# Batched fp32 matmul: groups of two matrices under automatic scheduling, against groups of four in hand-written engine programs with hardware loops

## The chip, the cores and the metric

One core of a Trainium2 chip. The metric is the device time of one execution in microseconds (us), as a median over runs. Ratios are the mean time of one kernel's fast runs over that of the other's in the same rounds, so they are not quite the ratio of the medians quoted beside them. "Span" is the time from the first to the last instruction in the profiled execution; the measured time is about 2 us longer.

## The reference

```python
b1, b2, m, k, n = 8, 16, 256, 512, 384
x:      (8, 16, 256, 512) float32
weight: (8, 16, 512, 384) float32
out = np.matmul(x, weight)          # 128 independent products, float32
```

168 MB are read and 50 MB written. The kernels cast to bf16 on the chip.

## The kernel before

It takes two matrices at a time (G = 2). A partition holds R = 4 consecutive rows of x of the pair, an 8 KB run. VectorE casts x to bf16, TensorE transposes it (two bf16 as one 4-byte word), VectorE copies the transposed x out of PSUM. Because each partition holds several rows, a product comes out with the matrices interleaved over partition blocks, and ScalarE needs G copies per matrix to put it in the order of the output.

```python
G = 2
C = P // G;  R = G * M // P;  J = R // G
LAG = 4                                   # stores kept back, in groups
...
def load_x(b):
    x_sb = x_pool.tile([P, R, K], fp32, name="x_sb")
    nc.sync.dma_start(x_sb[:], x_rows[b*M:(b+G)*M].rearrange("(p r) k -> p r k", r=R))
...
for b in range(0, B, G):
    last = b == B - G
    x_sb = load_x(b);  w_sb = [load_w(b + i) for i in range(G)]
    if last:
        while waiting: store()            # the kept stores go out behind the last loads
    x_t = transpose_x(x_sb)
    for i in range(G):
        ... cast of w, 8 matmuls into po ...
        mine = slice(i * C, (i + 1) * C)
        for g in range(G):
            nc.scalar.copy(out=out_sb[mine, g::G, :], in_=po[g*C:(g+1)*C, :, :N])
        if last: ... one store per matrix ...
    if not last: ... append; if len(waiting) > LAG: store() ...
```

## Time and profile before

| | before |
|---|---|
| time, median of 4 runs | 526.38 us (526.18 to 526.95) |
| span of the profiled run | 524.2 us |
| DMA share and rate, 20 to 500 us | 1.01, 423 GB/s |
| busiest compute engine | TensorE, 62% |
| data packets and semaphore packets | 36,880 |

How to read it: a share of 1.01 of 16 DMA engines means that by the records every engine has a packet under way all the time. The kernel is as fast as its DMA, plus a head in which nothing has arrived and a tail in which the last results are made and stored. The page lines for this are in the prediction below. One pair of views is shown here, because the prediction took a number from the first that the second contradicts. The first is the chain of waits at the end (start, length, what), the second VectorE's timeline in the same microseconds (start, length, what, and in brackets the idle time before and what ended it).

```profile
495.89 14.54 DMA w_sb<-in_weight_dram
510.44 0.01 issue
510.45 0.80 ACT out_sb L126
511.25 3.98 issue
```

```profile
510.21 1.23 DVE L76 CAST x_bf<-x_sb 128x2048 bf16<-128x2048 f32 x1 [3.17 <-DMA x_sb<-in_x_dram]
512.06 0.96 DVE L113 CAST w_bf<-w_sb 128x1536 bf16<-128x1536 f32 x1 [0.62 <-DMA w_sb<-in_weight_dram]
512.93 1.28 DVE L85 COPY x_t<-pt 128x1024 bf16<-128x1024 bf16 x2
514.13 0.95 DVE L113 CAST w_bf<-w_sb 128x1536 bf16<-128x1536 f32 x1
```

The chain's last DMA piece ends at 510.43. But the second view has VectorE waiting for the last **x** until 510.21, and for a weight until 512.06, with one more weight cast after that. Both weights of a group are queued behind its x, so what landed near 510 was the last x (at 510.11 us by the records of DMA completions), not the last weight.

### The profile page before, as it was taken

The page shows a single profiled execution, that of the slowest core. Times are in us where ns is not written, and L with a number is a line of the kernel's source. Part 1 is how long each engine was busy: PE and PEld are TensorE (multiplying, and loading weights), DVE is VectorE, ACT ScalarE, POOL GpSimd, SP SyncE. Part 2 cuts the span into 40 slices and gives each one's busy share as a digit, 9 for nine tenths or more (in the row PEclk, how much of TensorE's full clock was granted, in tenths as well). Part 3 has the DMA queues.
Part 4 walks back from the last instruction along what each step waited for, and adds up shares of the span by engine and source line. Part 5 has one row for each costly group of instructions (what it writes and reads, how often), then busy time and mean ns, then how long its engine had stood idle before and what let it go on. Part 6 is the DMA issues. An engine that isn't in the chain of part 4 may idle for free.

```text
span 524.2 us, 4635 instructions
## 1 busy us (share of the span) xinstructions
PE 324.2 (62%) x1536; PEld 187.1 (36%) x1536; DVE 272.8 (52%) x320; ACT 204.4 (39%) x257; POOL 0.7 (0%) x6
## 2 busy tenths in 40 slices
PE   4665665666655666657666565576646756757653
PEld 2443343333333433334333333343333433423331
DVE  4656455464554544645546456454464554645542
ACT  1462434434334343343343443424334334243342
POOL 0000000000000000000000000000000000000000
PEclk9898788887888878888788888877898888788788
DMA  8999999999999999999999999999999999999997
GB/s 342 421 414 418 421 424 422 424 422 422 425 423 421 422 422 423 423 423 422 424 422 424 421 424 424 420 425 424 424 426 424 420 425 424 425 422 425 424 423 258
DMA packets 36903, 218.40 MB, mean 417 GB/s; under 512 B 4113, under 2 KB 4113, under 8 KB 28689
## 3 DMA queue, kind: packets, MB, share of 16 engines
q1 hardware_dynamic: 36880, 218.12, 100.2%
q8 instruction: 12, 0.20, 0.1%
q14 instruction: 11, 0.08, 0.0%
HBM read 167.77 MB, written 50.33 MB: 416 GB/s over the span
## 4 chain that ended last, share of the span: by engine, by line
DMA 97%; issue 1%; ACT 1%; SPq 0%; ACTq 0%
DMA w_sb<-in_weight_dram 94%; DMA x_sb<-in_x_dram 3%; ACT out_sb L126 1%; ACTq L162 0%; SPq L66 0%; SPq L59 0%
## 5 line engine op out<-in xcount | busy, mean ns | idle before, releaser
L126 ACT COPY out_sb<-po 64x768 f32<-64x768 f32 x256 | 203.2, 794 | 313.3 <-issue 274.1
L117 PE MATMUL po<-w_bf,x_t 128*128 128x384 bf16 x1024 | 232.5, 390 | 48.1 <-DVE x_t L85 38.1
L76 DVE CAST x_bf<-x_sb 128x2048 bf16<-128x2048 f32 x64 | 78.5, 1227 | 199.0 <-DMA x_sb<-in_x_dram 199.0
L81 PE MATMUL pt<-identity,x_bf 128*128 128x128 f32 x512 | 92.2, 335 | 144.3 <-DVE x_bf L76 144.3
L117 PEld LDWEIGHTS <-x_t 128*128 128x128 bf16 x1024 | 109.7, 114 | 163.2 <-DVE x_t L85 60.1
L113 DVE CAST w_bf<-w_sb 128x1536 bf16<-128x1536 f32 x128 | 121.9, 955 | 38.6 <-DMA w_sb<-in_weight_dram 38.6
L81 PEld LDWEIGHTS pt<-identity,x_bf 128*128 128x128 f32 x512 | 77.4, 213 | 166.0 <-issue 164.9
L85 DVE COPY x_t<-pt 128x1024 bf16<-128x1024 bf16 x128 | 82.7, 684 | 4.8 <-PE pt L81 4.8
L126 ACT ACT_TABLE_LOAD x1 | 1.3, 1283 | 0.7 <-PEq L151 0.7
masks.py:199 POOL TENSOR_SCALAR_AFFINE_SELECT identity<-identity 128x128 f32<-128x128 f32 x1 | 0.3, 293 | 0.1
masks.py:197 POOL MEMSET identity<- 128x128 f32 x1 | 0.2, 204 | 0.3 <-POOLq L151 0.3
L151 POOL MEMSET const-bfloat16-1.0<- 128x1 bf16 x1 | 0.1, 102 | 0.0
L151 POOL MEMSET const-uint8-127<- 128x1 uint8 x1 | 0.1, 102 | 0.0
L151 POOL MEMSET const-float32-0.0<- 128x1 f32 x1 | 0.1, 99 | 0.2 <-issue 0.2
L151 POOL MEMSET const-float32-1.0<- 128x1 f32 x1 | 0.1, 99 | 0.0
## 6 DMA issues: line engine op xcount, KB each, us to landing
w_sb<-in_weight_dram SPq DMA_DIRECT2D x128, 768.0 KB, 16.1
x_sb<-in_x_dram SPq DMA_DIRECT2D x64, 1024.0 KB, 16.1
out_dram<-out_sb SPq DMA_DIRECT2D x63, 768.0 KB, 16.1
out_dram<-out_sb SPq DMA_DIRECT2D x2, 384.0 KB, 5.1
```

What stands on the lines that cost most here:

```text
L76: nc.vector.tensor_copy(out=x_bf[:, r0 : r0 + 4], in_=x_sb[:, r0 : r0 + 4])
L81: nc.tensor.transpose(pt[:, rr, h, :], words[:, r + rr, h :: KO // 2], identity)
L85: nc.vector.tensor_copy(out=x_t[:, j, :, :, g : g + 2].rearrange("k h i g c e -> k g (h i) (c e)"), in_=pt[:].bitcast(bf16).rearrange("k g ...
L113: nc.vector.tensor_copy(out=w_bf[:], in_=w_sb[i][:])
L117: nc.tensor.matmul(po[:, j, :N], x_t[:, j, ko // 2, i, :, :, ko % 2].rearrange("k g c -> k (g c)"), w_bf[:, ko, :], start=(ko == 0), stop= ...
L126: nc.scalar.copy(out=out_sb[mine, g::G, :], in_=po[g * C : (g + 1) * C, :, :N])
L151: nc = _bacc.Bacc("TRN2", target_bir_lowering=False, num_devices=1)
```

## The change

The intent: fewer and longer DMA packets (16 KB rows of x, 12 KB rows of out), a short program in hardware loops, and one engine, ScalarE, for all copies of results out of PSUM. The price that was known beforehand: four copies per matrix instead of two. The diff, cut to its core (each engine gets its own program, ordered by semaphores that count):

```diff
-    G = 2
+    G = 4                       # R = 8 rows per partition: 16 KB of x, 12 KB of out
     C = P // G
     R = G * M // P
-    LAG = 4
+    AHEAD = 2                   # groups of loads ahead
+    XS, WS, OS = AHEAD, AHEAD * G, 4
+    PT, PO = 4, 2               # PSUM: transposes, products (before 2 and 3)
...
+    def load(e, n, n0):
+        wait(e, x_cast, n - XS + 1)
+        e.dma_start(x_sb[n0 % XS][:], ...).then_inc(x_in[n0 % XS], 16)
+        for i in range(G):
+            wait(e, w_cast, n * G + (i + 1 - WS))
+            e.dma_start(w_sb[(n0 * G + i) % WS][:], ...).then_inc(...)
+    def store(e, n, n0):
+        e.wait_ge(o_copied, n * G + G)
+        e.dma_start(out=..., in_=out_sb[n0 % OS][:]).then_inc(o_out[n0 % OS], 16)
...
+    def copy_out(e, n, n0, t):                       # ScalarE
+        wait(e, o_out[n0 % OS], t * 16)
+        for i in range(G):
+            e.wait_ge(p_made, n * G + (i + 1))
+            for g in range(G):
+                ins = e.copy(out=out_sb[n0 % OS][i*C:(i+1)*C, g::G, :],
+                             in_=po[(n0*G + i) % PO][g*C:(g+1)*C, :, :N])
+            ins.then_inc(o_copied, 1)
...
+    @block.sync
+    def _(e):
+        for n in range(AHEAD): load(e, n, n)
+        with e.Fori(0, rounds) as t:
+            for s in range(U):
+                load(e, t * U + (AHEAD + s), AHEAD + s)
+                store(e, t * U + s, s)
+        for n in range(rounds * U, NG):
+            if n + AHEAD < NG: load(e, n + AHEAD, n + AHEAD)
+            store(e, n, n)
```

VectorE's program for a group is: cast x (one instruction), cast the first weight, four copies of transposed x, cast the other three weights. TensorE's is: 16 transposes, then four products. The special treatment of the last group (kept stores, one store per matrix) is gone.

More of the change, by code (lines that the diff above doesn't have):

```diff
@@ L27 @@
     x_rows = x.rearrange("b1 b2 m k -> (b1 b2 m) k")
+    w_rows = weight.rearrange("b1 b2 k n -> (b1 b2 k) n")
     o_rows = out.rearrange("b1 b2 m n -> (b1 b2 m) n")
-    w_flat = weight.rearrange("b1 b2 k n -> (b1 b2) k n")
     fp32 = mybir.dt.float32
     bf16 = mybir.dt.bfloat16
-    G = 2
+    G = 4
     C = P // G
@@ L39 @@
     J = R // G
-    LAG = 4
-    const = ctx.enter_context(tc.tile_pool(name="const", bufs=1))
-    x_pool = ctx.enter_context(tc.tile_pool(name="x_pool", bufs=3))
-    xb_pool = ctx.enter_context(tc.tile_pool(name="xb_pool", bufs=2))
-    xt_pool = ctx.enter_context(tc.tile_pool(name="xt_pool", bufs=2))
-    w_pool = ctx.enter_context(tc.tile_pool(name="w_pool", bufs=6))
-    wb_pool = ctx.enter_context(tc.tile_pool(name="wb_pool", bufs=4))
-    out_pool = ctx.enter_context(tc.tile_pool(name="out_pool", bufs=7))
@@ L50 @@
-    psum_t = ctx.enter_context(tc.tile_pool(name="psum_t", bufs=2, space=bass.MemoryType.PSUM))
-    psum_o = ctx.enter_context(tc.tile_pool(name="psum_o", bufs=3, space=bass.MemoryType.PSUM))
-    identity = const.tile([P, P], fp32)
-    make_identity(nc, identity)
-    def load_x(b):
-        x_sb = x_pool.tile([P, R, K], fp32, name="x_sb")
-        nc.sync.dma_start(
-            x_sb[:], x_rows[b * M : (b + G) * M].rearrange("(p r) k -> p r k", r=R)
-        )
-        return x_sb
-    def load_w(b):
-        w_sb = w_pool.tile([P, KO, N], fp32, name="w_sb")
-        nc.sync.dma_start(w_sb[:], w_flat[b].rearrange("(kp ko) n -> kp ko n", ko=KO))
-        return w_sb
@@ L69, in transpose_x @@
-    def transpose_x(x_sb):
-        x_bf = xb_pool.tile([P, R, K], bf16, name="x_bf")
-        x_t = xt_pool.tile([P, J, KO // 2, G, G, C, 2], bf16, name="x_t")
-        words = x_bf[:].bitcast(fp32)
-        for r0 in range(0, R, 4):
-            nc.vector.tensor_copy(out=x_bf[:, r0 : r0 + 4], in_=x_sb[:, r0 : r0 + 4])
-            for r in range(r0, r0 + 4, 2):
-                pt = psum_t.tile([P, 2, KO // 2, P], fp32, name="pt")
-                for rr in range(2):
-                    for h in range(KO // 2):
-                        nc.tensor.transpose(
-                            pt[:, rr, h, :], words[:, r + rr, h :: KO // 2], identity
-                        )
-                j, g = divmod(r, G)
-                nc.vector.tensor_copy(
-                    out=x_t[:, j, :, :, g : g + 2].rearrange(
-                        "k h i g c e -> k g (h i) (c e)"
-                    ),
-                    in_=pt[:].bitcast(bf16).rearrange(
-                        "k g h (i ce) -> k g (h i) ce", i=G
-                    ),
-                )
-        return x_t
@@ L95 @@
-    waiting = []
-    def store():
-        dram, out_sb = waiting.pop(0)
-        nc.sync.dma_start(out=dram, in_=out_sb)
-    for b in range(0, B, G):
-        last = b == B - G
-        x_sb = load_x(b)
-        w_sb = [load_w(b + i) for i in range(G)]
-        if last:
-            while waiting:
-                store()
-        x_t = transpose_x(x_sb)
-        out_sb = out_pool.tile([P, R, N], fp32, name="out_sb")
-        for i in range(G):
-            w_bf = wb_pool.tile([P, KO, N], bf16, name="w_bf")
-            nc.vector.tensor_copy(out=w_bf[:], in_=w_sb[i][:])
-            po = psum_o.tile([P, J, 512], fp32, name="po")
+    NG = B // G
@@ new lines, with sbuf, psum, sems @@
+    AHEAD = 2
+    XS, WS, OS = AHEAD, AHEAD * G, 4
+    BS, TS, WBS = 2, 2, 4
+    PT, PO = 4, 2
+    ctx.enter_context(tc.tile_critical())
+    def sbuf(name, shape, dtype, n):
+        return [
+            ctx.enter_context(nc.sbuf_tensor(f"{name}{s}", shape, dtype)) for s in range(n)
+        ]
+    def psum(name, shape, dtype, n):
+        return [
+            ctx.enter_context(nc.psum_tensor(f"{name}{s}", shape, dtype)) for s in range(n)
+        ]
+    def sems(name, n):
+        return [tc.alloc_semaphore(f"{name}{s}") for s in range(n)]
@@ new lines @@
+    identity = sbuf("identity", [P, P], fp32, 1)[0]
+    x_sb = sbuf("x_sb", [P, R, K], fp32, XS)
+    x_bf = sbuf("x_bf", [P, R, K], bf16, BS)
+    x_t = sbuf("x_t", [P, J, KO // 2, G, G, C, 2], bf16, TS)
+    w_sb = sbuf("w_sb", [P, KO, N], fp32, WS)
+    w_bf = sbuf("w_bf", [P, KO, N], bf16, WBS)
+    out_sb = sbuf("out_sb", [P, R, N], fp32, OS)
+    pt = psum("pt", [P, 2, KO // 2, P], fp32, PT)
+    po = psum("po", [P, J, 512], fp32, PO)
+    x_in, w_in, o_out = sems("x_in", XS), sems("w_in", WS), sems("o_out", OS)
@@ new lines, with wait @@
+    id_done, x_cast, w_cast, t_copied, t_made, p_made, o_copied = (
+        sems(name, 1)[0]
+        for name in (
+            "id_done", "x_cast", "w_cast", "t_copied", "t_made", "p_made", "o_copied"
+        )
+    )
+    T = R // 2
+    def wait(e, sem, value):
+        if not isinstance(value, int) or value > 0:
+            e.wait_ge(sem, value)
+    def load(e, n, n0):
+        wait(e, x_cast, n - XS + 1)
+        e.dma_start(
+            x_sb[n0 % XS][:],
+            x_rows[bass.ds(n * (G * M), G * M)].rearrange("(p r) k -> p r k", r=R),
+        ).then_inc(x_in[n0 % XS], 16)
+        for i in range(G):
+            wait(e, w_cast, n * G + (i + 1 - WS))
+            e.dma_start(
+                w_sb[(n0 * G + i) % WS][:],
+                w_rows[bass.ds(n * (G * K) + i * K, K)].rearrange(
+                    "(p ko) n -> p ko n", ko=KO
+                ),
+            ).then_inc(w_in[(n0 * G + i) % WS], 16)
@@ new lines, in store, with cast, cast_w @@
+    def store(e, n, n0):
+        e.wait_ge(o_copied, n * G + G)
+        e.dma_start(
+            out=o_rows[bass.ds(n * (G * M), G * M)].rearrange("(p r) n -> p r n", r=R),
+            in_=out_sb[n0 % OS][:],
+        ).then_inc(o_out[n0 % OS], 16)
+    def cast(e, n, n0, t):
+        e.wait_ge(x_in[n0 % XS], t * 16)
+        wait(e, t_made, n * T + (1 - BS) * T)
+        e.tensor_copy(out=x_bf[n0 % BS][:], in_=x_sb[n0 % XS][:]).then_inc(x_cast, 1)
+        def cast_w(i):
+            e.wait_ge(w_in[(n0 * G + i) % WS], t * 16)
+            wait(e, p_made, n * G + (i + 1 - WBS))
+            e.tensor_copy(
+                out=w_bf[(n0 * G + i) % WBS][:], in_=w_sb[(n0 * G + i) % WS][:]
+            ).then_inc(w_cast, 1)
+        cast_w(0)
+        wait(e, p_made, n * G + (1 - TS) * G)
+        for q in range(T):
+            e.wait_ge(t_made, n * T + (q + 1))
+            j, g = divmod(2 * q, G)
+            e.tensor_copy(
+                out=x_t[n0 % TS][:, j, :, :, g : g + 2].rearrange(
+                    "k h i g c e -> k g (h i) (c e)"
+                ),
+                in_=pt[(n0 * T + q) % PT][:].bitcast(bf16).rearrange(
+                    "k g h (i ce) -> k g (h i) ce", i=G
+                ),
+            ).then_inc(t_copied, 1)
+        for i in range(1, G):
+            cast_w(i)
@@ new lines, in multiply @@
+    def multiply(e, n, n0):
+        words = x_bf[n0 % BS][:].bitcast(fp32)
+        e.wait_ge(x_cast, n + 1)
+        for q in range(T):
+            wait(e, t_copied, n * T + (q + 1 - PT))
+            for rr in range(2):
+                for h in range(KO // 2):
+                    ins = e.transpose(
+                        pt[(n0 * T + q) % PT][:, rr, h, :],
+                        words[:, 2 * q + rr, h :: KO // 2],
+                        identity[:],
+                    )
+            ins.then_inc(t_made, 1)
+        e.wait_ge(t_copied, n * T + T)
+        for i in range(G):
+            e.wait_ge(w_cast, n * G + (i + 1))
+            wait(e, o_copied, n * G + (i + 1 - PO))
@@ L115 @@
             for j in range(J):
                 for ko in range(KO):
-                    nc.tensor.matmul(
-                        po[:, j, :N],
-                        x_t[:, j, ko // 2, i, :, :, ko % 2].rearrange("k g c -> k (g c)"),
-                        w_bf[:, ko, :],
+                    ins = e.matmul(
+                        po[(n0 * G + i) % PO][:, j, :N],
+                        x_t[n0 % TS][:, j, ko // 2, i, :, :, ko % 2].rearrange(
+                            "k g c -> k (g c)"
+                        ),
+                        w_bf[(n0 * G + i) % WBS][:, ko, :],
@@ L123 @@
                     )
-            mine = slice(i * C, (i + 1) * C)
-            for g in range(G):
-                nc.scalar.copy(out=out_sb[mine, g::G, :], in_=po[g * C : (g + 1) * C, :, :N])
-            if last:
-                waiting.append((o_rows[(b + i) * M : (b + i + 1) * M].rearrange(
-                    "(p r) n -> p r n", r=R), out_sb[mine]))
-                store()
-        if not last:
-            waiting.append(
-                (o_rows[b * M : (b + G) * M].rearrange("(p r) n -> p r n", r=R), out_sb[:])
-            )
-            if len(waiting) > LAG:
-                store()
+            ins.then_inc(p_made, 1)
@@ new lines, in copy_out @@
+    def copy_out(e, n, n0, t):
+        wait(e, o_out[n0 % OS], t * 16)
+        for i in range(G):
+            e.wait_ge(p_made, n * G + (i + 1))
+            for g in range(G):
+                ins = e.copy(
+                    out=out_sb[n0 % OS][i * C : (i + 1) * C, g::G, :],
+                    in_=po[(n0 * G + i) % PO][g * C : (g + 1) * C, :, :N],
+                )
+            ins.then_inc(o_copied, 1)
+    block = ctx.enter_context(nc.Block())
+    @block.gpsimd
+    def _(e):
+        e.memset(identity[:], 0.0).then_inc(id_done, 1)
+        e.wait_ge(id_done, 1)
+        make_identity(nc, identity[:], nomemset=True)
+        e.drain().then_inc(id_done, 1)
@@ new lines, in _ @@
+    @block.sync
+    def _(e):
+        U = OS
+        for n in range(AHEAD):
+            load(e, n, n)
+        rounds = (NG - AHEAD) // U
+        with e.Fori(0, rounds) as t:
[3 more added lines that the diff above has]
+        for n in range(rounds * U, NG):
+            if n + AHEAD < NG:
+                load(e, n + AHEAD, n + AHEAD)
+            store(e, n, n)
+        for s in range(OS):
+            e.wait_ge(o_out[s], 16 * (NG // OS))
@@ new lines, in _ @@
+    @block.vector
+    def _(e):
+        U = XS
+        for n in range(U):
+            cast(e, n, n, 1)
+        with e.Fori(1, NG // U) as t:
+            for s in range(U):
+                cast(e, t * U + s, s, t + 1)
+    @block.tensor
+    def _(e):
+        U = 4
+        e.wait_ge(id_done, 2)
+        for n in range(U):
+            multiply(e, n, n)
+        with e.Fori(1, NG // U) as t:
+            for s in range(U):
+                multiply(e, t * U + s, s)
+    @block.scalar
+    def _(e):
+        U = OS
+        for n in range(U):
+            copy_out(e, n, n, 0)
+        with e.Fori(1, NG // U) as t:
+            for s in range(U):
+                copy_out(e, t * U + s, s, t)
```

## The prediction

> **What bounds the kernel now.** I read the page first: the busy line, the slices, the DMA queues, the chain that ended last.
>
> ```profile
> PE 324.2 (62%) x1536; PEld 187.1 (36%) x1536; DVE 272.8 (52%) x320; ACT 204.4 (39%) x257; POOL 0.7 (0%) x6
> ...
> DMA  8999999999999999999999999999999999999997
> ...
> DMA packets 36903, 218.40 MB, mean 417 GB/s; under 512 B 4113, under 2 KB 4113, under 8 KB 28689
> ...
> q1 hardware_dynamic: 36880, 218.12, 100.2%
> ...
> DMA w_sb<-in_weight_dram 94%; DMA x_sb<-in_x_dram 3%; ACT out_sb L126 1%; ACTq L162 0%; SPq L66 0%; SPq L59 0%
> ```
>
> No compute engine is busy for more than 62% of the span, the 16 DMA engines are full in all slices but the first and the last, and 97% of the chain is loads. So the bound is the time of the DMA engines. The view by stage says how much is not steady state; its columns are length, busy time of PE, PEld, DVE, ACT, POOL, then granted clock, DMA share, GB/s.
>
> ```profile
> 0.00:2.00 2.00, 0.00 (x0) 0.00 (x0) 0.00 (x0) 1.27 (x1) 0.70 (x6) 1.00 0.21 25
> 2.00:510.50 508.50, 320.10 (x1512) 184.71 (x1512) 268.81 (x316) 199.26 (x253) 0.00 (x0) 0.85 1.01 422
> 510.50:517.00 6.50, 4.13 (x24) 2.42 (x24) 3.96 (x5) 2.48 (x4) 0.00 (x0) 1.00 0.94 390
> 517.00:524.20 7.20, 0.00 (x0) 0.00 (x0) 0.00 (x0) 1.44 (x2) 0.00 (x0) 0.78 0.53 150
> ```
>
> 508.5 of 524.2 us run at 422 GB/s. The head costs 2 us. The last weight lands at 510.45 us (chain in order of time), so the tail is 13.75 us; DMA is near full until 517, because four groups of stores were kept back for it, and half idle after.
>
> **What the Trainium skill says.** "HBM Reference", section Access: one core streaming alone measures about 425 GB/s, bounded by its 16 DMA engines. The trace agrees: 422. So only cheaper packets could speed the steady part up. "DMA: Bandwidth & Descriptors", section Why small descriptors are slow, gives each packet a fixed overhead of about 3 cycles. The trace shows such a term but larger: in its packet records the median of the 6144 B packets is 234 ns, of the 8192 B packets 309 ns, of the 4 B semaphore packets 9 ns. That is 75 ns per 2 KB and 9 ns fixed, whatever the size. "ScalarE: Activation LUTs", section What ACT_TABLE_LOAD costs, times an instruction as 186 ns + 0.833 ns per element of the free size, with no term for partitions; 768 elements would be 826 ns, less some 93 ns of overlap. The trace has 794 ns for 64x768. "Runtime: NRT & Kernel Launch", section Instruction fetch mechanics: instructions come in 16 KB blocks by DMA, and a taken branch to a block outside the window waits for a fetch. The trace has 12 instruction packets of 16 KB, of about 1.04 us each, and no loop.
>
> **The change, part by part.**
>
> Packets. Per four matrices and DMA engine, before: 16 x packets of 8 KB, 32 w of 6 KB, 16 out of 6 KB, 8 semaphore packets, 72 in all. After: 8 of 16 KB, 32 of 6 KB, 8 of 12 KB, 6 semaphores, 54. The bytes are the same. What is a fixed packet cost in throughput? Casts of x start 8.06 us apart (median of the trace), so 16.12 us per four matrices; the bytes alone are 2 x 104 units of 2 KB x 75 ns = 15.60 us; the rest, 0.52 us over 72 packets, is 7.2 ns. Eighteen fewer packets save 0.13 us, giving 15.99 us. Times 32: **-4.2 us**, 0.8%. If a 16 KB row were split into 8 KB packets, only 10 of the 18 would go and the saving would be 2.3 us; 16 KB instruction packets in this trace speak against a split.
>
> ScalarE.
>
> ```profile
> L126 ACT COPY out_sb<-po 64x768 f32<-64x768 f32 x256 | 203.2, 794 | 313.3 <-issue 274.1
> L117 PE MATMUL po<-w_bf,x_t 128*128 128x384 bf16 x1024 | 232.5, 390 | 48.1 <-DVE x_t L85 38.1
> L113 DVE CAST w_bf<-w_sb 128x1536 bf16<-128x1536 f32 x128 | 121.9, 955 | 38.6 <-DMA w_sb<-in_weight_dram 38.6
> ```
>
> With four matrices interleaved, a result leaves PSUM in four copies of 32x768, not two of 64x768. The free size is unchanged, so I take 794 ns each (0.805 apart, from 3.22 us for four in the timeline): 512 copies, 407 us, 12.9 us of each 16 us. ScalarE doubles to 77% busy and still fits. VectorE work is the same but with one cast per eight rows: from 955 ns at 1536 and 1227 ns at 2048 elements, 0.53 ns per element plus 139, so 2.31 us for 4096.
>
> Does the DMA stay fed? Times from the landing of a group's x: cast to 2.4; first weight cast to 3.4; four transposed copies at 684 ns to 6.1; first product at about 7.9; ScalarE's 16 copies to **20.8**. SyncE issues the store then, and the next group's loads behind it. In the queue at that moment lie the rest of the next group's weights, one store and a whole group of loads: the second next group ends landing at 2 x 16 + 7.4 = 39.5, so about **18 us of work are queued**. At the start, with three groups of loads and no stores, the margin is about 11 us. The wait for the store in front of the loads is therefore hidden. The loops' register work and branches lie on engines with idle time: hidden too, except in head and tail.
>
> Tail. The last weight lands at T. Before T go all loads and 29 of 32 stores (45.6 MB) against 59 of 64 (46.4 MB) now: -1.9 us. T = 510.45 - 1.9 - 4.0 = 504.6; I add 0.5 us for the entry into the blocks: 505. The last x landed 7.5 us before T, so by the same steps ScalarE ends at T + 13.3: 12.9 us of copies start just after T, because x_t was ready then. Two held stores fill the DMA to about T + 7.4, then it idles. The final 1.57 MB goes out in one piece. Now:
>
> ```profile
> 515.23 3.22 ACT L126 COPY out_sb<-po 64x768 f32<-64x768 f32 x4 [3.98 <-issue]
> ...
> 516.86 2.09 SPq L99 DMA_DIRECT2D out_dram<-out_sb  x2
> ```
>
> The last store of 0.39 MB was issued at 518.48 and the program ended 5.7 us later; its data took some 2 us. The new one needs 3.7 us of data (8 packets x 459 ns): about 7.7 us. Tail: 13.3 + 7.7 = **21 us** against 13.75, so **+7.3**.
>
> Sum: -4.2 +0.2 (part of the saving falls after T) -1.9 +7.3 +0.5 head +1 for leaving the block and for semaphore and register instructions in the last group = +2.9. Span 527; the measured time is 2.3 us above the span, so about 529 us.
>
> **The rivals.** (1) ScalarE becomes the bound. For it: 77% by my sum, only two PSUM buffers, so TensorE waits for it. Against: 12.9 of 16 us even when nothing overlaps within a group. It takes 25% more per copy to bind; then 32 x 16.1 and more, 535 to 550. (2) SyncE's wait for the store starves the loads. For it: one in-order queue. Against: the 18 us of margin; it needs a group's latency to double. Would be 540 or more. (3) The loops' branches refetch instructions by DMA. TensorE's loop is some 500 instructions, two or three blocks, seven times round: 14 to 21 blocks for the 12 of now. That adds little (0.6 us of one DMA engine each), but if all engines refetched and the fetches fell on one DMA engine, 5 to 15 us: up to 540. (4) The packet saving is larger or the DMA is fed more evenly, since the eight outstanding transfers of now (issue to landing 16.1 us for every kind, two groups) no longer limit it: at most about 5 us more, 522 to 525. DMA is already over 100% busy, so little is to be had. (5) The tail is shorter because ScalarE starts earlier than T; one or two us.
>
> **Range and chances.** Gain and loss are both below 1.5% and nearly cancel. The bytes at a pure 75 ns per 2 KB take 499 us, and head and new tail add some 20, so faster by 2% (under 516) is close to impossible. Slower by 2% (over 537) needs rival 1, 2 or 3. I put the time at 529.0 us, eight in ten between 522 and 537, 0.02 faster, 0.87 same, 0.11 slower.
>
> **What would show it.** Right: about 27,650 data and semaphore packets; 16 KB packets of about 609 and 12 KB ones of about 459 ns; x casts 15.9 to 16.1 us apart; DMA digits 9 but at the ends; 512 copies of about 794 ns; a last weight landing near 505 and a tail of about 21 us with DMA idle in its middle. Wrong: copies shorter or longer than 794 ns; DMA digits below 9 in mid-run; SyncE waiting on ScalarE with an empty queue; many more instruction packets; x casts at 16.1 or above in spite of fewer packets (then the packet cost overlaps and the saving is nil, 533).

## The result, and the profile after

532.06 us (median of 4; 531.13 to 532.20) against 526.38: ratio 1.0102, 95% interval 1.0085 to 1.0120. The time lies inside the range, but the loss is 5.7 us where +2.6 had been said (529.0 less 526.38).

The page of the changed kernel: engines, slices, packets, queue, ScalarE's copies.

```profile
PE 322.8 (61%) x1536; PEld 192.4 (36%) x1536; DVE 269.2 (51%) x288; ACT 405.5 (76%) x513; POOL 0.7 (0%) x6
...
DMA  8999999999999999999999999999999999999972
...
DMA packets 27655, 218.19 MB, mean 411 GB/s; under 512 B 3073, under 2 KB 3073, under 8 KB 19457
...
q1 hardware_dynamic: 27648, 218.12, 98.2%
...
L180 ACT COPY out_sb<-po 32x768 f32<-32x768 f32 x512 | 404.2, 789 | 117.1 <-PE po L163 110.1
```

What to see: ScalarE's work doubled as worked out (512 copies of 789 ns) and it still waits 110 us for TensorE; the DMA engines are full until the last two slices. Those two are at 7 and 2 tenths; before it was one slice at 7. So ScalarE did not become the bound of the steady part. SyncE waits long for ScalarE, but the DMA queue never runs dry in mid-run:

```profile
SPq L110 <- ACT out_sb L180: 226.2, 32, 16.6
```

That is 226 us of waiting in an in-order queue that costs nothing until the end; the backlog covers it, as the issue-to-landing time of 26 to 27 us per load (16.1 before) also says.

Now the end. By the trace's records of DMA completions, the last weight landed at **513.83 us** before and at **509.32 us** after. With the stages cut there (length, busy PE, PEld, DVE, ACT, POOL, clock, DMA share, GB/s), first before:

```profile
2.00:513.80 511.80, 321.42 (x1521) 185.86 (x1522) 271.48 (x319) 200.00 (x253) 0.00 (x0) 0.85 1.01 422
513.80:524.20 10.40, 2.81 (x16) 1.27 (x14) 1.28 (x2) 3.17 (x4) 0.00 (x0) 0.85 0.63 215
```

and after:

```profile
2.00:509.30 507.30, 315.97 (x1506) 189.31 (x1507) 266.97 (x286) 391.78 (x497) 0.00 (x0) 0.80 1.01 424
509.30:513.00 3.70, 2.59 (x16) 1.36 (x14) 2.20 (x3) 2.35 (x3) 0.00 (x0) 1.00 0.91 389
513.00:523.50 10.50, 4.25 (x16) 1.76 (x16) 0.00 (x0) 10.28 (x14) 0.00 (x0) 0.61 0.04 18
523.50:530.20 6.70, 0.00 (x0) 0.00 (x0) 0.00 (x0) 0.00 (x0) 0.00 (x0) 0.50 0.56 235
```

Before, the last weight is followed by 10.4 us. After, by 20.9 us: 3.7 in which the queue drains, **10.5 in which the DMA engines stand idle** (share 0.04) while ScalarE is busy for 10.28 of 10.50 us, and 6.7 for the last store. The gain up to the last weight is 4.5 us, the loss behind it 10.6; the span grows by 6.1 us. The packet records say what the 4.5 us are. Up to the last weight, 48.1 MB of stores had gone out before the change and 47.05 MB after it (bytes moved by then, less the loads), which at 422 GB/s are 2.4 us that were only moved behind the last weight. From the first packet on, bytes moved at 421.6 GB/s before and 423.5 after, which over 214.8 MB is a true gain of 2.3 us. The first packet came 0.2 us later. ScalarE's part of the tail is one line of its timeline, and the store that waits for it is the second of the two issues merged in SyncE's line:

```profile
510.63 12.84 ACT L180 COPY out_sb<-po 32x768 f32<-32x768 f32 x16 [3.52 <-PE po L163]
...
507.14 16.69 SPq L110 DMA_DIRECT2D out_dram<-out_sb  x2
```

The other half of the change can be read from the packet records: medians of 611 ns for 16 KB and 460 ns for 12 KB packets (609 and 459 had been worked out), and 3 instruction packets of 16 KB in place of 12.

### The profile page after: what moved, and what is told of

Same layout as the page of the kernel before. It is cut to its first block, busy times and chain, and to the rows that moved or that the text cites. A ratio compares the mean times of both kernels' runs of the same rounds, so it can differ in the third digit from the quotient of the medians.

```text
span 530.3 us, 5467 instructions
## 1 busy us (share of the span) xinstructions
PE 322.8 (61%) x1536; PEld 192.4 (36%) x1536; DVE 269.2 (51%) x288; ACT 405.5 (76%) x513; POOL 0.7 (0%) x6
## 4 chain that ended last, share of the span: by engine, by line
DMA 50%; ACT 23%; PE 9%; issue 8%; DVE 7%; SPq 1%; ACTq 0%; DVEq 0%
DMA x_sb<-in_x_dram 50%; ACT out_sb L180 23%; PE pt L151 5%; DVE x_bf L119 5%; PE po L163 4%; DVE x_t L133 2%; SPq L110 1%; ACTq _compat.py:109 0%; DVE w_bf L124 0%; SPq L95 0%; DVEq L90 0%; SPq L201 0%; DVEq L131 0%; ACTq L236 0%; ACTq L178 0%
## 5 line engine op out<-in xcount | busy, mean ns | idle before, releaser
L180 ACT COPY out_sb<-po 32x768 f32<-32x768 f32 x512 | 404.2, 789 | 117.1 <-PE po L163 110.1
L163 PE MATMUL po<-w_bf,x_t 128*128 128x384 bf16 x1024 | 226.9, 379 | 142.1 <-ACT out_sb L180 108.8
L163 PEld LDWEIGHTS po<-w_bf,x_t 128*128 128x128 bf16 x1024 | 104.8, 109 | 255.7 <-issue 204.2
L119 DVE CAST x_bf<-x_sb 128x4096 bf16<-128x4096 f32 x32 | 73.4, 2294 | 220.8 <-DMA x_sb<-in_x_dram 220.8
L151 PE MATMUL pt<-identity,x_bf 128*128 128x128 f32 x512 | 96.2, 364 | 55.0 <-DVE x_bf L119 55.0
L124 DVE CAST w_bf<-w_sb 128x1536 bf16<-128x1536 f32 x128 | 116.7, 953 | 0.0
L151 PEld LDWEIGHTS pt<-identity,x_bf 128*128 128x128 f32 x512 | 87.6, 218 | 71.1 <-issue 69.6
L133 DVE COPY x_t<-pt 128x1024 bf16<-128x1024 bf16 x128 | 84.5, 688 | 21.5 <-PE pt L151 20.9
```

What stands on the lines that cost most here:

```text
L119: e.tensor_copy(out=x_bf[n0 % BS][:], in_=x_sb[n0 % XS][:]).then_inc(x_cast, 1)
L124: e.tensor_copy(out=w_bf[(n0 * G + i) % WBS][:], in_=w_sb[(n0 * G + i) % WS][:]).then_inc(w_cast, 1)
L133: e.tensor_copy(out=x_t[n0 % TS][:, j, :, :, g : g + 2].rearrange("k h i g c e -> k g (h i) (c e)"), in_=pt[(n0 * T + q) % PT][:].bitcast( ...
L151: ins = e.transpose(pt[(n0 * T + q) % PT][:, rr, h, :], words[:, 2 * q + rr, h :: KO // 2], identity[:],)
L163: ins = e.matmul(po[(n0 * G + i) % PO][:, j, :N], x_t[n0 % TS][:, j, ko // 2, i, :, :, ko % 2].rearrange("k g c -> k (g c)"), w_bf[(n0 * G ...
L180: ins = e.copy(out=out_sb[n0 % OS][i * C : (i + 1) * C, g::G, :], in_=po[(n0 * G + i) % PO][g * C : (g + 1) * C, :, :N],)
```

## The experiments

The theories. **P**: a packet costs some 7 ns of DMA throughput, so fewer packets explain the gain up to the last weight. Its rivals: **N**, the fixed part of a packet is hidden, since the median cadence of x casts (the time from the start of one to the start of the next) barely fell (2 x 8.06 = 16.12 to 16.11 us per four matrices); and **F**, the gain comes from the loops, as instruction packets disappear. **T**: the loss is the new tail, ScalarE's copies and then the undivided store. Its rival **D**: the drain of the queue or the chain from the last x sets the end anyway.

| run | time, us | ratio to before | last weight landed | last copy ended | span |
|---|---|---|---|---|---|
| r_after | 531.14 | 1.0091 | 508.91 | 522.77 | 529.57 |
| e_unrolled | 531.65 | 1.0106 | 508.80 | 522.32 | 529.57 |
| e_pk72 | 536.07 | 1.0181 | 512.39 | 527.77 | 534.66 |
| e_pk144 | 550.04 | 1.0452 | 527.43 | 540.22 | 547.26 |
| t_split | 529.87 | 1.0062 | 509.21 | 523.16 | 528.12 |
| t_share | 528.09 | 1.0033 | 509.21 | 519.03 | 525.87 |
| t_xearly | 533.13 | 1.0130 | 509.16 | 524.65 | 531.46 |
| t_share_x | 529.00 | 1.0054 | 509.07 | 520.15 | 526.99 |
| b_order | 527.37 | 1.0016 | 509.45 | 519.03 | 525.87 |
| b_share_split | 525.74 | 0.9993 | 509.04 | 518.75 | 523.75 |
| b_share_split_2 | 525.43 | 0.9983 | 509.17 | 517.99 | 523.00 |
| b_final | 526.38 | 0.9988 | 509.39 | 519.46 | 524.47 |

The columns of landings and copies are from each run's profile. Half-widths of the ratios' 95% intervals are 0.0013 to 0.0019. All results were correct.

### The changed kernel again, and its loops unrolled

> The changed kernel again, as the base for the runs beside it: 531 to 532.2 us, cadence of the x casts 16.11 us, last weights landing near 509.3 us.

> The changed kernel with its loops unrolled, nothing else. Theory F (the hardware loops give the steady part its gain, because the instruction packets of 16 KB stop: 12 before, 3 after): 12 or more such packets come back and with them single steps of the x casts 0.4 to 0.8 us longer than the median of 16.11; the time grows by 2 to 3 us to about 534.5. Rival (the fewer data packets give the gain, the loops give nothing): time within 0.7 us of the changed kernel, 532.

```diff
-        with e.Fori(1, NG // U) as t:
+        for t in range(1, NG // U):        # likewise in all four programs
```

r_after came out at the low end of what was expected: 531.14 us, cadence 16.08 us, last weight at 508.91 us. Unrolled, the instruction packets came back. These are both pages' lines for queue q8, whose 16 KB packets are taken here for TensorE's by their number (an inference), first with loops (r_after), then unrolled:

```profile
q8 instruction: 3, 0.05, 0.0%
```

```profile
q8 instruction: 12, 0.20, 0.1%
```

The time moved by 0.5 us (by the ratios, 1.0106 against 1.0091, by 0.8 us, with intervals that overlap). **F falls at the size it claimed**, 2 to 3 us; an effect under 1 us is possible and not shown. The last weight landed at 508.80 us against 508.91, but with 0.45 MB fewer stores gone out before it: the rate up to there is 422.8 GB/s unrolled against 423.6, which is about 0.9 us, in one profile each. Two single steps of the x casts are 0.3 to 0.4 us above 16.11 in the unrolled run; the profiled run of the changed kernel, with loops, has one such step too (16.53 us), so they are no proof of a cost of fetches.

### The old packet sizes in the new kernel, and half of them

> The changed kernel with each x load in two transfers of 8 KB runs and each store in two of 6 KB runs: 72 packets per four matrices and engine as before the change, not 54. Theory P of the prediction (a packet costs 7.2 ns of throughput): 18 x 7.2 ns x 32 = +4.2 us, about 536. Rival N (the fixed part of a packet overlaps its neighbour, since the cadence fell only from 16.12 to 16.11): under +1 us, about 532.5.

> The changed kernel with x in four transfers of 4 KB runs, each weight in two of 3 KB runs, each store in four of 3 KB runs: 144 packets per four matrices and engine. Theory P: 90 x 7.2 ns x 32 = +20.7 us, about 553. Rival N: under +5 us, below 537.

```diff
-        e.dma_start(x_sb[n0 % XS][:], ...).then_inc(x_in[n0 % XS], 16)
+        for a in range(0, R, R // XP):     # XP, WP, OP = 2, 1, 2 or 4, 2, 4
+            e.dma_start(x_sb[n0 % XS][:, a : a + R // XP], ...).then_inc(x_in[n0 % XS], 16)
         # likewise each weight in WP and each store in OP transfers; waits for 16 * XP and so on
```

The queue line of e_pk72 and of e_pk144 (packets, MB, share):

```profile
q1 hardware_dynamic: 36864, 218.12, 98.1%
```

```profile
q1 hardware_dynamic: 73728, 218.14, 100.1%
```

The bytes are the same, the packets 1.33 and 2.67 times r_after's 27,648. The time rose by 4.9 and 18.9 us; P had said 4.2 and 20.7, N under 1 and under 5. **P holds, N falls.** The landing of the last weight gives the cost without the tail: 3.5 us for 18 x 32 packets per engine is 6.0 ns, 18.5 us for 90 x 32 is 6.4 ns. The cadence of the x casts (median 16.08, 16.23, 16.66 us) gives 8.3 ns for the first step, too coarse to use, and 6.5 ns over the whole.

But 0.4 MB more of stores went out before the last weight in both runs than in r_after. The rate from the first packet to the last weight leaves that out: 423.6 GB/s in r_after, 421.5 in e_pk72, 409.5 in e_pk144, which over r_after's 214.7 MB is 4.4 and 6.1 ns. So a packet cost **some 4 to 6.5 ns** between 3 and 16 KB, not 7.2. The packet records agree in kind: medians of 121 ns (3 KB), 159 (4 KB), 236 (6 KB), 460 (12 KB) and 611 (16 KB) are 75.4 ns per 2 KB and some 8 ns fixed. And with the packets and transfers of the kernel before, the new kernel falls back to that kernel's rate, 421.5 against 421.6 GB/s: they explain the whole gain in rate. The packet count includes the semaphore packets, and the number of transfers rose with it (192 in r_after, 256 and 512), so these runs do not separate the two. The rest of e_pk72's loss, some 1.4 us, lies behind the last weight.

N had leaned on the median cadence of the kernel before. Its mean is longer than its median: 8.106 us against 8.062 from the sixth cast on, because of single steps of up to 8.9 us. Twice the mean is 16.21, close to e_pk72's 16.23. What makes those long steps in the kernel before was not settled: some have an instruction packet within them, others of its instruction packets come without one, and the unrolled run has two.

### The tail: the store in parts, the copies on two engines

> The changed kernel with the last group's store in four parts, each as soon as its matrix is copied. Theory T (the new tail is ScalarE's 16 copies, 12.9 us, and then the store): ScalarE ends as before, about 21.4 us after the last x; only 0.39 MB of the store are left then, so the time falls by 1 to 2.5 us, to about 529.5. Rival D (the tail is the drain of the queue and the store's size matters fully): falls by 3 us or more.

```diff
+    def store_last(e, n, n0):
+        for i in range(G):
+            e.wait_ge(o_copied, n * G + i + 1)
+            e.dma_start(out=<matrix i>, in_=out_sb[n0 % OS][i*C:(i+1)*C]).then_inc(...)
```

As T expected: the last copy ends at 523.16 us, about where it did (522.77 in r_after), and the last store lands 3.3 us after it in place of 5.1 (527.89 in r_after). The time is 529.87 us, 1.3 us under r_after, and D's 3 us or more did not come. The intervals of the two ratios just touch (1.0046 to 1.0077, 1.0074 to 1.0108), but the slowest of the four runs (529.96 us) is under the fastest of r_after (530.61).

> The changed kernel with VectorE taking half of the last group's copies out of PSUM, every other group as it was. Theory T: the last copy ends 5 to 6 us earlier (VectorE is free only after the last weight cast), the store and the end follow: about 526. Rival D (queue drain or the x chain in front sets the end): less than 2 us.

```diff
+        if n == LAST:                                  # VectorE, behind its last weight cast
+            for i in range(G):
+                e.wait_ge(p_made, n * G + (i + 1))
+                for g in range(HALF, G):               # HALF = 2; ScalarE does the others
+                    ins = e.tensor_copy(out=out_sb[n % OS][i*C:(i+1)*C, g::G, :], in_=po[...])
+                ins.then_inc(o_shared, 1)
# store and TensorE wait for o_shared too; the last round of the loops is unrolled
```

The time fell by 3.0 us, the last copy by 3.7 us. Between T's 5 to 6 and D's "less than 2": the direction is T's, and D falls, but the size was too hopeful. The timeline of t_share's last group shows why:

```profile
508.50 2.69 DVE L129 CAST w_bf<-w_sb 128x1536 bf16<-128x1536 f32 x3
...
510.20 3.21 ACT L197 COPY out_sb<-po 32x768 f32<-32x768 f32 x4 [3.48 <-PE po L180]
511.22 7.81 DVE L153 COPY out_sb<-po 32x768 f32<-32x768 f32 x8
```

VectorE is busy with the weight casts until 511.2, one microsecond after ScalarE has begun, and takes 976 ns for such a copy (7.81 us for eight) where ScalarE's start 803 ns apart (3.21 us for four). TensorE needs the PSUM buffers that VectorE empties, so ScalarE now waits for VectorE through TensorE.

### The last x earlier: a miss, and two more

> The changed kernel with the last group's x loaded ahead of the weights of the group before it. Theory T: ScalarE starts on the last group when it is done with the group before, 2 to 3.5 us earlier than now, and the end moves by as much: about 528.5. If the last group's start did not matter, no change: 531.

> Both together. Theory T: the copies end near the time when the two stores held in the queue have drained (about 7.5 us after the last weight), so the DMA engines run through to the last store; span about 522.5, time about 524.5, a little under the kernel before. If the DMA engines still stand idle before the last store, 526 or more.

```diff
+            if n + AHEAD == NG - 2:
+                load_x(e, NG - 2, NG - 2)
+                load_x(e, NG - 1, NG - 1)      # ahead of the weights of group NG - 2
```

Both missed: t_xearly is 2.0 us **slower** than r_after, t_share_x 0.9 us slower than t_share. VectorE's timeline of t_xearly, in the group before the last (group 30 of 0 to 31):

```profile
485.78 2.29 DVE L125 CAST x_bf<-x_sb 128x4096 bf16<-128x4096 f32 x1 [7.76 <-DMA x_sb<-in_x_dram]
492.56 0.96 DVE L130 CAST w_bf<-w_sb 128x1536 bf16<-128x1536 f32 x1 [4.49 <-DMA w_sb<-in_weight_dram]
493.44 2.48 DVE L139 COPY x_t<-pt 128x1024 bf16<-128x1024 bf16 x4
```

The weights of this group now come 4.9 us later than in t_share (the first at 492.45 us against 487.58), behind the extra x. VectorE works in order, its first weight cast stands before the copies of transposed x, and so these wait 4.49 us for a weight that they do not need. ScalarE's two last groups then run without a gap from 498.91 to 524.65, 32 copies on end. The expectation had moved the x and forgotten what was queued behind it.

> Shared copies and the early last x, and in the last two groups VectorE copies the transposed x out before the first weight cast, not after. Theory T, with the cause of the miss of the early x seen in its trace (VectorE, in order, held the transposed copies behind a weight that had not landed): group 30 starts on ScalarE near 495 us instead of 498.9, the last copy ends near 516, when the queue has drained, the last store lands near 520.5; span 522 to 523.5, time about 524.5, 0.3% under the kernel before. Rival (the order costs as much elsewhere): 528 or more.

```diff
-        cast_w(0)                              # in the last two groups:
-        ... four copies of transposed x ...
+        ... four copies of transposed x ...
+        cast_w(0)
```

This took the wait away (527.37 us, 1.6 us under t_share_x), but is only 0.7 us under t_share, and its last copy ends at 519.03 like t_share's, not at 516. Group 30 still starts on ScalarE at 496.6 us, not 495: its first weight landed at 492.7 us, and its first product took 2.8 us from its start to the first copy, at a granted TensorE clock of 0.50 (493.8 to 496.4 us), where t_share's took 1.6; its third and fourth products wait for PSUM that ScalarE has to free; and the last group's transposes stand behind those in TensorE's order, at 504.5 us. The early x bought no gain clear of noise (0.7 us under t_share).

### A version that beats both, barely

> Shared copies in the last group and its store in four parts. Theory T: both gains add up, about 1.3 us under the run with shared copies alone, 526.8; if the store's parts only overlap the drain of the queue, no gain over it, 528.

> The run with shared copies and split store once more, with more rounds: 525.7 us, 0.1 to 0.2% under the kernel before, within its noise.

Shared copies and the split store add up: 525.74 and 525.43 us, ratios 0.9993 (0.9974 to 1.0012) and 0.9983 (0.9969 to 0.9996). The store's four parts in the second of them go out between 512.19 and 518.38 us, as the copies end, while in r_after the one store waited until 522.8:

```profile
512.19 6.19 SPq L115 DMA_DIRECT2D out_dram<-out_sb  x4
```

That is 5.7 us under r_after and 0.2% under the kernel before. Only the second run's interval excludes 1, and only just. The two gains had been expected to sum to 4.3 us; why it is more was not tested, and the runs were in different jobs. A part of the tail no edit sets: the two profiles of this one kernel differ by 0.8 us in the last copy, as the last group's 16 transposes took 3.59 us in the first, at a granted clock of 0.58 (504 to 508 us), and 2.18 us in the second, at 1.00.

> Shared copies and split store as in the run before, and the last group's x in two transfers and two casts, so that its transposes begin with the first half, its weights cast between them, ScalarE taking 9 of the 16 copies. Theory T: ScalarE starts about 2.6 us earlier, near 507.3 us, the last copy ends near 516 us; span about 521.5, time about 523.3, 0.6% under the kernel before. Rival (the queue's drain near 516.5 us has become the limit of the tail): no gain beyond 1 us, 525.

```diff
+        half(0, x_half, 16, h_cast)            # last group: x in two loads and two casts
+        turned(0);  half(1, ...);  turned(1);  cast_w(0);  turned(2);  turned(3)
```

A miss: 526.38 us, no better. The first half of x was cast at 499.55 us, 2.2 us earlier than before, but TensorE was not free:

```profile
500.52 2.72 PE L252 MATMUL po<-w_bf,x_t 128*128 128x384 bf16 x8 [1.00 <-ACT out_sb L269]
503.04 1.84 PE L238 MATMUL pt<-identity,x_bf 128*128 128x128 f32 x8
...
504.81 1.22 DVE L147 CAST x_bf<-x_sb 128x2048 bf16<-128x2048 f32 x1
```

The last product of group 30 waits for a PSUM buffer from ScalarE and ends at 503.2; the transposes come after it in TensorE's program. The second half of x had landed at 501.94 us, but its cast stands behind the first copy of transposed x in VectorE's program, which waits for those transposes, and so began only at 504.81. The first product then started at 508.74 us, 0.4 and 1.2 us later than in the two runs without the cut x, and took 2.8 us to its first copy, at a granted clock of 0.57 (508 to 512 us), where theirs took 1.6. So the early start was lost to TensorE's order, VectorE's order and the clock, and neither theory's number came out. This is read from one profile, that of the slowest of the five runs (524.96 to 527.44 us); no run tested it.

## Why the prediction was right or wrong

- **What bounds the kernel: right.** DMA is full in the steady part of every run.
- **ScalarE: right.** 512 copies of 789 ns against 794 assumed, 76% against 77%; no bound in the steady part.
- **Hidden wait for the store: right.** 226 us of SyncE waiting, no dip of the DMA slices.
- **Packets: right mechanism, size too large.** 4.0 us before the last weight had been said; the rates before and after give 2.3. One sign of being wrong did appear, casts of x 16.1 us apart, and the time was near the 533 us that went with it. But the saving was not nil: the 16.12 to compare with was twice a median that leaves out long steps, and twice the mean is 16.21.
- **The rivals.** 1, 2 and 3 did not occur; of rival 3, the 14 to 21 refetched blocks did not come either, there were 3 in all. Nor did 4, since the rate rose by no more than the packets explain, or 5, since ScalarE began at 510.63 us, 1.3 us after the last weight.
- **Where it failed: "The last weight lands at 510.45 us (chain in order of time), so the tail is 13.75 us".** The landing was 513.83 us and the old tail 10.35 us. The number was taken from an inferred link of the chain; VectorE's timeline, shown above, has the last x landing at that time. The step enters twice: as the start of T and as the tail to compare with.

| term, us | predicted | measured |
|---|---|---|
| last weight lands, before | 510.45 | 513.83 |
| packets, before the last weight | -4.0 | -2.3 (421.6 to 423.5 GB/s) |
| stores moved behind the last weight | -1.9 | -2.4 (48.1 to 47.05 MB) |
| start of the program | +0.5 | +0.2 (first packet 1.79 to 2.00) |
| last weight lands, after | 505 | 509.32 |
| from there to ScalarE's last copy | 13.3 | 14.15 |
| from there to the end (7.7, and 1 for leaving) | 8.7 | 6.8 |
| tail after, the sum of these two | 22 | 20.95 |
| tail before | 13.75 | 10.35 |
| change of the span | +2.9 | +6.1 |

With 513.83 in its place, the same steps give 513.83 - 1.9 - 4.0 + 0.5 = 508.4 for the last weight and 530.4 for the end; the profile has 530.3. That this fits so well is luck: the last weight came 0.9 us later than 508.4, ScalarE's end another 0.85 us later, and the last store with the end took 1.9 us less. For ScalarE's 0.85 us the trace has the last group's transposes, 3.68 us at a granted clock of 0.50 (504 to 508 us), 2.18 us where it was 1.00 (b_share_split_2). The 0.5 and 1 us for entering and leaving the blocks rested on no measurement. Small slips that did not matter: 5.7 us less 2 plus 3.7 is 7.4, not 7.7; rival 3 counts 0.6 us for an instruction packet that took 1.04; and the figure of 425 GB/s stands in the section Specifications (TRN2) of "HBM Reference" (the prediction named another).

The old tail was better than the prediction thought: it had kept four groups of stores for the DMA engines to do, and a last group half as large. No run gave these two back to the new kernel, so their shares are not shown. Of the new tail, t_split shows 1.3 us to be the undivided store, t_share 3.0 us the copies on one engine alone, and both together 5.7 us (531.14 to 525.43; the runs were in different jobs). In b_share_split the tail is still 14.7 us (509.04 to 523.75) against 10.35 before, and eats the gain of the packets again.

## What to carry to other kernels

In a kernel bound by DMA, larger groups pay a few nanoseconds per packet saved in the steady part (here 4 to 6.5) and charge a whole group's latency once, at the end; add up both before choosing, and give the last group a shared form and a store in parts (5.7 us here; a smaller last group was not tried). Date the start of the tail by what consumes the last load, or by its completion record, and not by the last DMA piece of an inferred chain. Before moving a load forward, look at what is queued behind it, on the DMA queue and in the in-order engines that wait for it.

## What the Trainium skill lacked or had wrong

- "DMA: Bandwidth & Descriptors", section Why small descriptors are slow, gives about 3 cycles of fixed overhead per packet and speaks of small packets. In these runs packets of 3 to 16 KB still cost 4 to 6.5 ns each of throughput (8 to 9 ns in the packet records), and 90 packets more per group and DMA engine cost 3.6% of the time (531.14 to 550.04 us).
- "Runtime: NRT & Kernel Launch", section Instruction fetch mechanics, warns that a taken branch to a block outside the window waits for a fetch, and gives no cost for a loop that stays inside it. Here no 16 KB block was fetched after 127 us with the loops (r_after): 3 in all, against 12 unrolled, and unrolling cost 0.5 us, within noise. This does not contradict the page.
- "ScalarE: Activation LUTs", section What ACT_TABLE_LOAD costs, names no dependence on partitions. The runs confirm that there is none to speak of: 794 ns for 64x768, 789 ns for 32x768, so a result that leaves in copies of half the partitions costs twice the time.
- No page that was used here says that the chain of waits in a profile can end in a DMA piece that the work did not wait for; here it was 3.4 us off (510.43 against 513.83 us).
